# Loading a page table as eight rows and spreading it with a TensorE transpose

## The chip, the cores and the metric

The kernel runs on one core of a Trainium2 chip. The metric is the device time of one execution in microseconds (us). Several executions are timed and their median is given; one more is recorded by the profiler, and that execution has a time and a span of its own. A core has five engines that work side by side, each in the order of its own instruction queue: TensorE (PE in the profile, and PEld for its loads of weights), VectorE (DVE), ScalarE (ACT), GpSimd (POOL) and SyncE (SP, which here only issues transfers). Sixteen DMA engines move the data.

## The reference

One layer of a decoder is computed for a prompt of 1024 tokens and for 8 sequences of 4 new tokens each. Every token goes through a normalisation with a shift and a scale that depend on its sequence, then through two branches: attention with a forget gate (8 heads of 64), and an mLSTM (4 heads of 128). The branches are merged, and an MLP of width 4096 follows. What the change touches is the attention of the 8 short sequences. Their past keys, values and forget gates lie in pages of 128 tokens, and a table says which pages belong to which sequence:

```python
page_table: (8, 4) int32          # 8 sequences, 4 pages each, values 0..39
k_past  = cache_k[layer][page_table].reshape(8, 512, 8, 64)
v_past  = cache_v[layer][page_table].reshape(8, 512, 8, 64)
lf_past = cache_logf[layer][page_table].reshape(8, 512, 8)
fk = cumsum(concatenate([lf_past, a_logf], axis=1), axis=1)   # enters the scores
```

## The kernel before

The kernel keeps the activations as columns (features on the 128 partitions, tokens along the row) and multiplies each weight tile with them in three passes, a high and a low part of each operand (`gemm`, lines 400 to 411). Line 406 multiplies high by high, 407 the high weight by the low activation, 408 the low weight by the high activation. `split_w` (lines 260 to 269) loads a weight tile on SP's queue (L263), makes its high part on ACT (L267) and its low part on DVE or POOL in turn (L268).

**The start.** First the conditioning is multiplied out (`ada_first`, L294, L275). Meanwhile nine tiles of x are loaded on SP's queue (`load_x`, L180) and normalised (`norm_x`: the square on ACT at L310, the rest on DVE and POOL, L312 to L315). `h_part` then transposes x on PE (L336), scales and shifts it out of PSUM on ACT (L341) or DVE (L339), and splits it into a high part on ACT (`Xh`, L348) and a low part on DVE (`Xl`, L349). The h of all tokens is made in three chunks of 352 tokens, each in two halves. The gate products and the first projections run on PE between these parts.

**The order.** The program is written as a sequence of stages: gates, `qkv(0)`, `dprep()`, and then for each of four pairs of heads the attention and the next `qkv`, with further products (`fill`) placed between. A planner lays out each engine's queue when the kernel is built: it goes by priorities that follow the order of the program, with offsets by name, and by a simulated timeline (`TCARGS`). Buffers of a tag go round in the order in which the program asks for them. Two tags matter here. `PT` has two buffers of SBUF; `h_part` uses them for its unsplit half, `dprep` for its two work tiles A and B, and attention for its transposed probabilities. `ps_t`, asked for with `bank("t")`, has two banks of PSUM; the transposes to tokens in `qkv` (L628, read by ACT at L629, and L632), the one in `dprep` (L577) and those of attention (L707, read at L709 and L710) use them in turn.

**`dprep`** turns the table into row numbers. The caches are seen as rows of which 32 (forget gates) or 64 (keys, values) make up a page, so that partition p, with j = p // 32 and r = p % 32, wants row 32 * table[b, j] + r for sequence b. In the kernel before, four loads on SP (L553) bring the table to all partitions, one for each page j: each writes column j of the table, 8 words, to 32 partitions. DVE casts them to float (L556), multiplies and adds the row number (L559), and writes three sets of indices (L560, L562). Eight lookups on POOL (`gather`, L440) then fetch the forget gates into A. A copy (L574), four transposes (L577), a running sum (L579) and some scaling (L578 to L583) end in `nF2`, which the decoding stage needs much later; its lookups of keys and values use the same indices.

Of the kernel before, what the change touches and what calls it, by code (L numbers as in the profile page):

```python
# [11 lines left out]
I32 = mybir.dt.int32  # L12
U32 = mybir.dt.uint32
AF = mybir.ActivationFunctionType
ALU = mybir.AluOpType
# [3 lines left out]
P = 128  # L19
D = 1024  # L20
NP = 1024
NB = 8
TD = 4
ND = NB * TD
T = NP + ND
# [20 lines left out]
PAGES = 4  # L46
# [16 lines left out]
def _mark(nc, label):  # L63
    pass
# [3 lines left out]
def hybrid_kernel(ctx: ExitStack, tc: tile.TileContext, ins, outs):  # L68
    nc = tc.nc
    pe, act, dve, pool, sp = nc.tensor, nc.scalar, nc.vector, nc.gpsimd, nc.sync  # L70
    uid = [0]

    def tl(pl, shape, dt=F32, tag=None, bufs=None):
        uid[0] += 1
        tag = tag or f"u{uid[0]}"
        kw = {} if bufs is None else {"bufs": bufs}
        return pl.tile(list(shape), dt, name=f"{tag}_{uid[0]}", tag=tag, **kw)
# [13 lines left out]
    def f(ap):  # L91
        return ap.bitcast(F32)

    def bc(ap, n):

        return ap.broadcast_to(list(ap.shape[:-1]) + [n])
# [43 lines left out]
    cst = ctx.enter_context(tc.tile_pool(name="cst", bufs=1))  # L140
# [9 lines left out]
    def slot(role, shape, dt=F32):  # L150

        uid[0] += 1
        n, w = {"Pt": (3, KEYS * 2), "PT": (2, T)}.get(role, (1, T))
        t = big.tile([P, w], dt, name=f"{role}_{uid[0]}", tag=role, bufs=n)
        m = 1
        for x in shape[1:]:
            m *= x
        t = t[:shape[0], 0:m]
        if len(shape) == 3:
            t = t.rearrange("p (a b) -> p a b", b=shape[2])  # L160
        elif len(shape) == 4:
            t = t.rearrange("p (a b c) -> p a b c", b=shape[2], c=shape[3])
        return t
# [3 lines left out]
    def bank(tag):  # L167
        return tl(ps, [P, 512], F32, "ps_" + tag, PSB[tag])
# [35 lines left out]
    ident = tl(cst, [P, P])  # L204
# [47 lines left out]
    pt = bank("t")  # L252
# [69 lines left out]
    def h_part(ci, q):  # L322
# [7 lines left out]
        for k in range(4 * q, 4 * q + 4):  # L330
# [15 lines left out]
            if k % 2:  # L346
                k2 = slice(k - 1, k + 1)
                act.copy(hh[:, k2], hf)  # L348
                dve.tensor_sub(hl[:, k2], hf, f(hh[:, k2]))  # L349

    def load_params():
        prow = slot("stg", [120, P])
        act.dma_start(prow[0:48], ins["b_ada"].rearrange("l (r p) -> (l r) p", p=P))
        for i, nm in enumerate(("g_pre_mix", "g_post_mix", "g_pre_mlp", "g_post_mlp")):
            act.dma_start(prow[48 + 8 * i:56 + 8 * i], ins[nm].rearrange("l (r p) -> (l r) p", p=P))
        act.dma_start(prow[80:112], ins["conv_w"].rearrange("l j (r p) -> (l j r) p", p=P))
        act.dma_start(prow[112:120], ins["conv_b"].rearrange("l (r p) -> (l r) p", p=P))
        pt = bank("t")
        pe.transpose(pt[:, :120], prow, ident[:120, :120])
        dve.tensor_copy(prm, pt[:, :120])  # L360
# [17 lines left out]
    for i in range(8):  # L378
        if i == 0:
            load_params()  # L380
        if i >= AW:
            ada_w.append(load_ada(i))
        ada_first(i)
        for _ in range(X_AT[i]):
            x_l.append(load_x(len(x_l)))
            if len(x_l) <= 3:
                norm_x(len(xts))
        for ci in HAT.get(i, ()):
            P_(f"h{ci}0", h_part, ci, 0)
            h_done.append((ci, 0))  # L390
        if i == GW:
            gate_w = P_("gw", load_gate_w)
# [46 lines left out]
    def gather(dst, src, i, b):  # L439
        pool.indirect_dma_start(dst, None, src, bass.IndirectOffsetOnAxis(idx[:, i, b:b + 1], 0))  # L440
# [51 lines left out]
    if True:  # L492
# [39 lines left out]
        for q in range(2):  # L532
            pt = bank("t")
# [6 lines left out]
        pt = bank("t")  # L540
# [5 lines left out]
    def dprep():  # L546

        _mark(nc, "dprep")
        pti = tl(cst, [P, NB], I32)
        rowi = tl(cst, [P, 1], I32)  # L550
        for j in range(PAGES):
            r_ = slice(32 * j, 32 * j + 32)
            sp.dma_start(pti[r_], ins["page_table"][:, j:j + 1].rearrange("b o -> o b").broadcast_to([32, NB]))  # L553
            pool.iota(rowi[r_], [[0, 1]], 0, 1)
        ptf = tl(cst, [P, NB])
        dve.tensor_copy(ptf, pti)  # L556
        rowf = tl(cst, [P, 1])
        dve.tensor_copy(rowf, rowi)
        dve.tensor_scalar(ptf, ptf, 32.0, rowf, ALU.mult, ALU.add)  # L559
        dve.tensor_copy(idx[:, 0], ptf)  # L560
        for i in range(2):
            dve.tensor_scalar(idx[:, 1 + i], ptf, 2.0, float(i), ALU.mult, ALU.add)  # L562

        A = slot("PT", [P, T])
        lfg = A[:, 0:256].rearrange("p (b c) -> p b c", b=NB)
        for b in range(NB):
            gather(lfg[:, b], clf, 0, b)
        lfh = A[:, 256:512].rearrange("p (i h b) -> p i h b", i=4, h=AH)
        nFd = A[:64, 512:512 + KEYS]
        B = slot("PT", [P, T])  # L570
        LR = B[:64, 0:PAST + TD]
        Fd = B[:64, PAST + TD:2 * (PAST + TD)]
        sp.dma_start(LR[:, PAST:], d_lfd.rearrange("h (b t) -> (h b) t", t=TD))
        dve.tensor_copy(lfh, lfg.rearrange("p b (i h) -> p i h b", i=4))  # L574
        pt = bank("t")
        for i in range(4):
            pe.transpose(pt[:64, i * P:(i + 1) * P], lfh[:, i].rearrange("p h b -> p (h b)"), ident)  # L577
        act.copy(LR[:, 0:PAST].rearrange("p (x i) -> p i x", i=4), pt[:64].rearrange("p (i x) -> p i x", i=4))  # L578
        dve.tensor_tensor_scan(Fd, bc(one[:64, 0:1], PAST + TD), LR, 0.0, ALU.mult, ALU.add)  # L579
        act.mul(nFd[:, 0:PAST].rearrange("p (i x) -> p i x", i=4), Fd[:, 0:PAST].rearrange("p (x i) -> p i x", i=4), -1.0)  # L580
        dve.tensor_scalar(nFd[:, PAST:].rearrange("p (b t) -> p b t", t=TD), Fd[:, PAST:].unsqueeze(1).broadcast_to([64, NB, TD]), -1.0, None, ALU.mult)
        act.copy(nF2[0:64], nFd)
        dve.tensor_sub(nF2[64:P], nFd, f(nF2[0:64]))  # L583
# [68 lines left out]

    nxt = qkv(0)
    dprep()
    for fp in range(4):
        heads = nxt
        KL = heads[2]
        _mark(nc, f"attn{fp}")
        if True:
            for hd in range(2):  # L660
# [7 lines left out]
                for j in range(4):  # L668
# [28 lines left out]
                    for m in range(j + 1):  # L697
                        pt = bank("t")
# [175 lines left out]
    if True:  # L874
# [298 lines left out]
        pt = bank("t")  # L1173
# [37 lines left out]
    for q in range(2):  # L1211
        pt = bank("t")
# [267 lines left out]
    for n_, (c, ts) in enumerate(((0, (0, 8, 1, 2, 3)), (1, (0, 8, 1, 2, 3)), (1, (4, 5, 6, 7)), (0, (4, 5, 6, 7)))):  # L1480
        if c not in W:
            W = {c: w_half(c)}
        for i, t in enumerate(ts):
# [4 lines left out]
            with after(last) if t == 8 else nullcontext():  # L1488
                o, last = R.gemm(W[c])
# [38 lines left out]
    def u_out(c, ft, h, eng):  # L1528
        if eng == "A":
            act.activation(c, c, AF.Relu)  # L1530
            act.activation(c, c, AF.Square)
        else:
            dve.scalar_tensor_tensor(c, c, 0.0, c, ALU.max, ALU.mult)
        sp.dma_start(d_u[ft, :, HB[h][0]:HB[h][1]], c)

    def pair(i, hs):
# [54 lines left out]
        for h in hs:  # L1591
            u_out(c1[h], 2 * i, h, "A")

# [155 lines left out]
```

## Time and profile before

| What | Value |
|---|---|
| Median of three runs | 1887.87 us (1885.29 to 1894.61) |
| The profiled execution's own time | 1890.58 us |
| Its span, from the first to the last instruction | 1888.6 us |
| PE busy | 1813.9 us (96% of the span) |
| DVE busy | 996.0 us (53%) |
| ACT busy | 819.6 us (43%) |
| POOL busy | 423.6 us (22%) |
| Mean granted clock of TensorE | 0.981 |
| Moved by DMA | 211.80 MB, mean 112 GB/s |

In the profile a line such as `DVE u L556 <- DMA u<-in_page_table: 10.9, 1, 10.9` says who waited (DVE, at line 556, writing a tile named u), for whom (a transfer from the page table), for how many microseconds in total, how often, and how long at the longest. Small constants have names of the form u and a number, and the profile shows them all as u. A row of a table by stretches has the busy time of PE, PEld, DVE, ACT and POOL in that stretch, each with its number of instructions, and then the clock that TensorE was granted (1.00 is full speed), the mean busy share of the sixteen DMA engines, and GB/s.

### The profile page before, as it was taken

To read this page: it belongs to the slowest core of one execution; us is meant where nothing else is said; L and a number is where in the kernel's file an instruction comes from. 1 tells how busy PE (TensorE), PEld (TensorE's weight loads), DVE (VectorE), ACT (ScalarE), POOL (GpSimd) and SP (SyncE) were. 2 spreads that over 40 slices of the span, in tenths; PEclk is the share of its full clock that TensorE was granted. 3 is DMA by queue.
4 is the path that set the end of the run, shared out by engine and by line. 5 is a ranking of instruction groups with operands and counts; after the bars stand their busy time and mean duration, and the time that the engine had idled before them with its cause. 6 is when DMAs were issued, how large, how long until landed. Compare 5 with 4: busy or idle time off the path is not lost. (4 is left out here: it accounts for less than half of the span.)

```text
span 1888.6 us, 29922 instructions
## 1 busy us (share of the span) xinstructions
PE 1813.9 (96%) x11871; PEld 1683.3 (89%) x11871; DVE 996.0 (53%) x1927; ACT 819.6 (43%) x1424; POOL 423.6 (22%) x337
## 2 busy tenths in 40 slices
PE   6899999999999999999999978999998999999997
PEld 3799789998888999979898767899998899999997
DVE  3554555554446555554454487756457424444436
ACT  4556546556556434443132666444445431111201
POOL 3200010000233111111143243444443211111113
PEclk9999999999999999989899988999999999999998
DMA  8321432122556312164234343433344522222223
GB/s 276 79 70 61 143 90 79 51 78 93 170 190 214 93 52 69 32 209 153 68 102 131 127 135 95 121 104 109 103 152 145 157 94 92 91 91 91 91 62 123
DMA packets 203381, 211.80 MB, mean 112 GB/s; under 512 B 14589, under 2 KB 170809, under 8 KB 203242
## 3 DMA queue, kind: packets, MB, share of 16 engines
q1 hardware_dynamic: 198154, 192.92, 32.3%
q0 software_dynamic: 4864, 16.91, 2.7%
q8 instruction: 93, 1.52, 0.3%
q14 instruction: 46, 0.38, 0.1%
q10 hardware_dynamic: 224, 0.06, 0.0%
HBM read 166.16 MB, written 43.70 MB: 111 GB/s over the span
## 5 line engine op out<-in xcount | busy, mean ns | idle before, releaser
L406 PE MATMUL ps_g<-Xh,wh 128*128 128x352 f32 (+1 forms) x1176 | 392.3, 334 | 0.2 <-ACT Xh L348 0.2
L408 PE MATMUL ps_g<-Xh,wl 128*128 128x352 f32 (+1 forms) x1176 | 389.4, 332 | 0.2 <-DVE wl L268 0.2
L407 PE MATMUL ps_g<-Xl,wh 128*128 128x352 f32 (+1 forms) x1080 | 355.0, 329 | 1.2 <-DVE Xl L349 1.1
L406 PEld LDWEIGHTS ps_g<-Xh,wh 128*128 128x128 f32 (+1 forms) x1176 | 221.8, 189 | 6.0 <-issue 3.0
L408 PEld LDWEIGHTS ps_g<-Xh,wl 128*128 128x128 f32 (+1 forms) x1176 | 220.9, 188 | 6.3 <-issue 4.5
L406 PE MATMUL ps_g<-R,wh 128*128 128x352 f32 x672 | 217.7, 324 | 1.8 <-ACT wh L1255 1.7
L408 PE MATMUL ps_g<-R,wl 128*128 128x352 f32 x672 | 218.5, 325 | 0.0
L407 PE MATMUL ps_g<-R,wh 128*128 128x352 f32 x672 | 217.6, 324 | 0.0
L407 PEld LDWEIGHTS ps_g<-Xl,wh 128*128 128x128 f32 (+1 forms) x1080 | 202.5, 188 | 7.3 <-issue 4.0
L268 POOL TENSOR_TENSOR wl<-wr,wh 128x1024 fp32r<-128x1024 f32 x26 | 62.7, 2410 | 433.1 <-ACT wh L267 371.9
L1647 DVE TENSOR_TENSOR acc<-acc,ps_g 128x352 f32<-128x352 f32 x144 | 74.6, 519 | 151.0 <-PE ps_g L408 151.0
L1256 POOL TENSOR_TENSOR wl<-wr,wh 128x1024 fp32r<-128x1024 f32 (+1 forms) x43 | 101.0, 2352 | 229.9 <-ACT wh L1255 223.6
L1255 ACT CAST wh<-wr 128x1024 fp32r<-128x1024 f32 (+1 forms) x63 | 61.2, 975 | 194.8 <-PE ps_g L407 148.0
L406 PEld LDWEIGHTS ps_g<-R,wh 128*128 128x128 f32 x672 | 126.2, 188 | 2.4 <-ACT wh L1255 1.9
L408 PEld LDWEIGHTS ps_g<-R,wl 128*128 128x128 f32 x672 | 126.5, 188 | 0.0
L407 PEld LDWEIGHTS ps_g<-R,wh 128*128 128x128 f32 x672 | 126.1, 188 | 0.0
L683 DVE CUSTOM_DVE_ANT_0 Pt<-ps_s,nF 128x384 f32<-128x384 f32 (+4 forms) x96 | 51.7, 554 | 65.2 <-PE ps_t L707 39.6
L267 ACT CAST wh<-wr 128x1024 fp32r<-128x1024 f32 x52 | 54.5, 1048 | 72.0 <-PE ps_g L407 54.1
L1256 POOL TENSOR_TENSOR wl<-wx,wh 128x512 fp32r<-128x512 f32 (+1 forms) x18 | 35.5, 1975 | 186.2 <-ACT wh L1255 184.5
L1255 ACT CAST wh<-S 128x1024 fp32r<-128x1024 f32 x44 | 46.3, 1052 | 40.3 <-PE ps_g L1519 17.9
L709 ACT CAST PT<-ps_t 128x512 fp32r<-128x512 f32 (+1 forms) x80 | 40.5, 545 | 53.1 <-PE ps_t L707 52.6
L690 ACT ACTIVATE Pt<-Pt,nm 128x128 f32<-128x128 f32 (+3 forms) x64 | 49.7, 777 | 31.8 <-DVE nm L688 20.8
(714 smaller groups left out, 4560.7 us busy)
## 6 DMA issues: line engine op xcount, KB each, us to landing
wr<-in_w_in SPq DMA_DIRECT2D x44, 512.0 KB
wr<-in_w_up SPq DMA_DIRECT2D x33, 512.0 KB
R<-d_u SPq DMA_DIRECT2D x32, 528.0 KB
wr<-in_w_ada SPq DMA_DIRECT2D x32, 512.0 KB
wr<-in_w_down SPq DMA_DIRECT2D x24, 512.0 KB
d_sg<-sgo SPq DMA_DIRECT2D x60, 176.0 KB
d_u<-n SPq DMA_DIRECT2D x32, 272.0 KB
d_u<-n SPq DMA_DIRECT2D x32, 256.0 KB
```

The lines of the kernel that those rows point to most:

```text
L267: act.copy(wh, wr)
L268: (dve if lo_turn[0] % 2 else pool).tensor_sub(wl, wr, f(wh))
L406: pe.matmul(o, wh[:, k], rh(k, a, b), start=(k == 0), stop=False)
L407: pe.matmul(o, wh[:, k], rl(k, a, b), start=False, stop=False)
L408: last = pe.matmul(o, wl[:, k], rh(k, a, b), start=False, stop=(k == nk - 1))
L683: dve.tensor_tensor_reduce(Pt[:, k0:k1], s_, nF[:, k0:k1], 1.0, -3.0e38, ALU.add, ALU.max, mx[:, pi:pi + 1])
L690: act.activation(Pt[:, :nk], Pt[:, :nk], AF.Exp, bias=nm, accum_out=sm)
L709: act.copy(PTh[:, :w_], pt[:, :w_])
L1255: act.copy(h_, src)
L1256: (pool if on_pool else dve).tensor_sub(l_, src, f(h_))
L1647: dve.tensor_tensor(accs[a // 352](ft), accs[a // 352](ft), o, ALU.add)
```

## The change

The table is loaded as it lies in memory, eight rows of four words, in one transfer on ACT's queue at the head of `load_params`. In `dprep` DVE casts it to float and repeats each of the four entries 32 times along the row, which gives 8 rows of 128 in the upper part of work tile A. A transpose on PE makes of this 128 partitions of 8, in a bank of the tag "t". The multiplication and addition reads that bank; the index operations behind it are as they were. The four loads and the cast behind them are gone. Work tile A is asked for earlier in the program, and one more "t" bank is asked for.

```diff
+    pg = tl(cst, [NB, PAGES], I32)
+
     def load_params():
+        act.dma_start(pg, ins["page_table"])
         prow = slot("stg", [120, P])
...
     def dprep():
-        pti = tl(cst, [P, NB], I32)
         rowi = tl(cst, [P, 1], I32)
         for j in range(PAGES):
             r_ = slice(32 * j, 32 * j + 32)
-            sp.dma_start(pti[r_], ins["page_table"][:, j:j + 1].rearrange("b o -> o b").broadcast_to([32, NB]))
             pool.iota(rowi[r_], [[0, 1]], 0, 1)
         ptf = tl(cst, [P, NB])
-        dve.tensor_copy(ptf, pti)
         rowf = tl(cst, [P, 1])
         dve.tensor_copy(rowf, rowi)
-        dve.tensor_scalar(ptf, ptf, 32.0, rowf, ALU.mult, ALU.add)
+        A = slot("PT", [P, T])
+        pgx = A[:NB, 900:900 + P]
+        dve.tensor_copy(pgx.rearrange("b (j r) -> b j r", r=32), bc(pg.unsqueeze(2), 32))
+        pt = bank("t")
+        pe.transpose(pt[:, 0:NB], pgx, ident[:NB, :NB])
+        dve.tensor_scalar(ptf, pt[:, 0:NB], 32.0, rowf, ALU.mult, ALU.add)
         dve.tensor_copy(idx[:, 0], ptf)
...
-        A = slot("PT", [P, T])
         lfg = A[:, 0:256].rearrange("p (b c) -> p b c", b=NB)
```

## The prediction

> **What bounds the kernel now.** I read the page first, for the shares of the engines.
>
> ```profile
> span 1888.6 us, 29922 instructions
> PE 1813.9 (96%) x11871; PEld 1683.3 (89%) x11871; DVE 996.0 (53%) x1927; ACT 819.6 (43%) x1424; POOL 423.6 (22%) x337
> ```
>
> PE is the bound: 1888.6 - 1813.9 = 74.7 us of the span are PE idle, and only what shortens these, or PE's work at a low clock, shortens the kernel. Then I cut the span into stretches of 60 us, to see where the idle time lies.
>
> ```profile
> 0.00:60.00 60.00, 37.09 (x184) 20.73 (x184) 22.66 (x61) 25.45 (x41) 16.65 (x39) 0.89 0.80 252
> 60.00:120.00 60.00, 58.69 (x365) 55.28 (x366) 37.85 (x79) 37.27 (x57) 14.37 (x12) 1.00 0.24 64
> 120.00:180.00 60.00, 60.00 (x373) 54.89 (x371) 29.54 (x83) 37.17 (x63) 2.39 (x1) 1.00 0.19 64
> ```
>
> The first column after the stretch is its length, the next PE's busy time; the last three are the granted clock, the DMA share and GB/s. The first 60 us hold 60 - 37.09 = 22.9 us of PE idle, more than any other stretch, and the page table is read there. From 60 us on PE is nearly never short of work. So I asked for the waits of the first 130 us, engine by engine (DVE's, PE's and ACT's own lists; total, times, longest).
>
> ```profile
> DVE u L556 <- DMA u<-in_page_table: 10.9, 1, 10.9
> PE ps_t L336 <- DVE PT L339: 7.6, 1, 7.6
> ACT stg L310 <- DMA Pt<-in_x_prompt: 9.5, 1, 9.5
> ```
>
> The three longest waits of the three engines are one event. The timeline of SP, DVE, PE and ACT (start, length, instruction, idle before it and its releaser) puts it in order:
>
> ```profile
> 37.97 1.26 SPq L263 DMA_DIRECT2D wr<-in_w_in  x2
> 39.28 2.88 SPq L553 DMA_DIRECT2D u<-in_page_table  x4
> 42.27 1.14 SPq L180 DMA_DIRECT2D Pt<-in_x_prompt  x2
> 43.46 5.12 SPq L180 DMA_DIRECT2D Pt<-in_x_sample  x1
> ...
> 54.01 0.17 DVE L556 CAST u<-u 128x8 f32<-128x8 int32 x1 [10.87 <-DMA u<-in_page_table]
> 54.12 0.64 DVE L339 TENSOR_SCALAR PT<-ps_t,mod,mod 128x352 f32<-128x352 f32 x1
> ...
> 46.88 0.33 PE L406 MATMUL ps_g<-Xh,wh 128*72 128x352 f32 x1
> 54.82 0.48 PE L336 MATMUL ps_t<-u,KB 128*128 128x128 f32 x1 [7.62 <-DVE PT L339]
> ...
> 44.95 1.17 ACT L341 ACTIVATE PT<-ps_s,mod,mod 128x352 f32<-128x352 f32 x2
> 55.67 1.06 ACT L310 ACTIVATE stg<-Pt 128x1024 f32<-128x1024 f32 x1 [9.54 <-DMA Pt<-in_x_prompt]
> ```
>
> DVE works in order. The cast of the page table (L556) stands in its queue at 43.1 us and waits 10.87 us. Behind it stand the two evacuations L339 of the transposed x; PE runs out at 47.2 and waits 7.62 us for them. ACT waits 9.54 us for a tile of x that SP issued just behind the page table. What the DMA did meanwhile:
>
> ```profile
> 39.00:43.00 4.00, 2.29 (x10) 1.69 (x10) 3.12 (x6) 3.18 (x7) 1.64 (x2) 0.50 1.05 254
> 43.00:50.00 7.00, 4.20 (x23) 3.34 (x21) 0.15 (x2) 2.54 (x4) 2.94 (x2) 0.89 0.08 7
> 50.00:54.00 4.00, 0.00 (x0) 0.00 (x0) 0.00 (x0) 0.00 (x0) 0.00 (x0) 0.67 0.76 233
> 54.00:58.00 4.00, 3.18 (x15) 2.80 (x15) 3.99 (x11) 2.33 (x4) 0.33 (x1) 0.50 0.64 139
> ```
>
> For 7 us, from 43 to 50, it moved 7 GB/s at a share of 0.08, which is about one of the sixteen engines, while the last piece of x stood in SP's queue with an issue of 5.12 us. That is the page table going over in single words, four loads of 256 words of 4 bytes, and x does not pass it. The clock then falls to 0.50 and PE restarts slowly.
>
> **The change, step by step.** *The four loads go.* They free 2.88 us of SP and the 7 us of nearly empty DMA. In their place one load of eight rows of 16 bytes goes out first on ACT's queue, at the start of the kernel; it is needed only after the h stage, so it is hidden. It delays ACT's queue by about one small issue of ACT's:
>
> ```profile
> 8.44 0.28 ACTq L364 DMA_DIRECT2D u<-in_b_fox_f  x1
> ```
>
> I take 0, with 0.3 us as the upper end, if a parameter load behind it should be on the path.
>
> The Trainium skill (DMA: Bandwidth & Descriptors, Rules for kernel authors) says that a last dimension which isn't contiguous is sent as one descriptor per element; the 7 us stretch agrees. The same page (Anatomy of one DMA) fits a DMA that GpSimd issues by 2.0 us plus bytes over 436 GB/s, and by that the four loads would have landed near 44 us, my estimate, and their removal would be worth about 1 us, a time near 1887. The 10.87 us of the row decide against it.
>
> *DVE's wait goes.* DVE runs L339 at 43.2 and PE finds its bank at 47.2: 7.62 us. What is late next is ACT, whose L348 cast stands behind L310, the square of the late tile of x. That tile is now issued at about 39.4 and follows the two weight tiles of 512 KB that SP issued at 37.97. How those landed:
>
> ```profile
> 42.36 1.05 ACT L267 CAST wh<-wr 128x1024 fp32r<-128x1024 f32 x1 [0.77 <-DMA wr<-in_w_in]
> 44.00 1.05 ACT L267 CAST wh<-wr 128x1024 fp32r<-128x1024 f32 x1 [0.59 <-DMA wr<-in_w_in]
> ```
>
> They came 44.00 - 42.36 = 1.64 us apart, so a third of this size lands at 45.6, before ACT is free (44.95 + 1.17 = 46.1), and ACT moves by its whole 9.54 us. The other end: in the profile the tile released ACT 5.7 us after the transfers had picked up again at 50; counted from 43.5 that gives 49.2, and a shift of 55.67 - 49.2 = 6.5 us. From 47 to 60 PE, ACT and DVE hand each other tiles of h, so the stage moves by ACT's shift, between 6.5 and 9.5; the words still draining explain part of the 5.7, so I stand nearer the weights' rows: 8.5 us. A PE that stays at full clock is counted in it, as its work there is not the last to end.
>
> *The index work moves.* New on DVE is one cast of 8 x 128, new on PE one transpose with 8 columns out; the two index operations behind them stay. Nearest rows:
>
> ```profile
> 112.41 0.23 PE L541 MATMUL ps_t<-u,stg 72*32 72x72 f32 x1
> 54.68 0.22 DVE L559 TENSOR_SCALAR u<-u,u 128x8 f32<-128x8 f32 x1
> ```
>
> The cast replaces a cast. PE pays 0.1 to 0.3, I take 0.2. POOL's four index rows stay.
>
> *The lookups start later.* This is the price that the profile doesn't show. The transpose takes a bank of the two "t" banks, which go round in program order: its turn comes after the token transposes of the first qkv, and its bank is the one that ACT's L629 gives back. So idx is ready only after that, and the eight lookups with it:
>
> ```profile
> 72.17 1.62 POOL L440 DMA_INDIRECT PT<-in_cache_logf,u  x1 [10.44 <-DVE Xl L349]
> 81.87 0.94 POOL L440 DMA_INDIRECT PT<-in_cache_logf,u  x1 [0.30 <-issue]
> 85.31 0.86 DVE L574 COPY PT<-PT 128x256 f32<-128x256 f32 x1 [1.97 <-DMA PT<-in_cache_logf,u]
> ...
> 121.71 1.08 ACT L629 COPY stg<-ps_t 128x512 f32<-128x512 f32 x2 [1.65 <-PE ps_t L628]
> 125.74 0.60 PE L577 MATMUL ps_t<-u,PT 128*64 128x128 f32 x4
> 130.81 0.47 ACT L709 CAST PT<-ps_t 128x384 fp32r<-128x384 f32 x1
> ```
>
> The first and the last of the eight are shown. On the clock of before: bank free at 121.71 + 1.08 = 122.8, transpose and three index operations to about 124, lookups and landing as now 85.31 - 72.17 = 13.1 us, copy 0.9: L577 at 138.0 in place of 125.74, 12.3 us late. Attention's first L709 writes the same PT buffer, and moves from 130.81 to about 139. Queued behind it on PE, ACT and DVE is the rest of the first head. The cover is the second qkv and the gate products: PE is busy for all 60 us of 120 to 180, POOL for 2.39 of them, so the eight lookups (about 10.6 us of POOL) find it free. With cover the delay costs PE nothing; without it, up to 12.3 us. Nothing excludes a small gain, as the lookups leave 72 to 83, but PE was full there: lower end 0. I take 1.3, for one wait in order on L574 and L577 of the size of the 1.97 us that L574 shows now: the fill is nearest, since the rows show full cover.
>
> *Sum.* The profiled execution took 1890.58 us, span 1888.6 and 2.0 around it. 1890.58 - 8.5 + 0.2 + 1.3 = 1883.6. It stands 2.7 above the median of the runs, 1887.87, so for a median I say 1881. The instruction order is laid out anew at build time, over the whole kernel, by a planner that works with a simulated timeline; I add +-4 us for that, an estimate from the 10.6 us that PE idles between 60 and 1080 and that a new order can make or lose in part:
>
> ```profile
> 60.00:1080.00 1020.00, 1009.37 (x6423) 911.53 (x6424) 539.11 (x1291) 502.69 (x917) 182.72 (x182) 0.99 0.34 106
> ```
>
> **Rivals.** *The lookups cost more than the stall (slower).* At 12.3 us with no cover: 1887.87 - 8.5 + 0.2 + 12.3 = 1892. It decides from the point where over 8.3 us of the delay arrive at the end of the kernel. For it: the fills are a fixed stock, and those run early are missing later. Against it: PE is full from 120 to 180, and the 1080 us stretch above has only 1% idle. Of a slowing of the lookups themselves, beside a busy DVE, the value lookups are the row:
>
> ```profile
> L440 POOL DMA_INDIRECT VB<-in_cache_v,u x5: 933/954/1469, 510.8 to 606.3; - x5
> ```
>
> min, median and max are 933, 954 and 1469 ns, against 0.95 us for most of the eight now: at the worst 8 x 0.5 = 4 us more, which makes 1896. The Trainium skill (SBUF — State Buffer, SBUF: two separate sides) tells of a transfer issued by GpSimd that grew from about 620 to 3100 ns beside a DVE copy; by five times, my estimate, the chain would be 30 us later still and the time over 1910. The medians do not bear that out, and I give it 1 in 100. All together 13 in 100.
>
> *More comes off.* All of DVE's 10.87 us, with a PE that never cools: 1887.87 - 10.87 - 1 = 1876. For it: PE runs at 0.50 from 54 to 58, 3.18 us of work that would take half. Against it: ACT's 9.54 is less. 17 in 100.
>
> *x is late anyway.* If ACT's tile comes no earlier, PE gets its bank at 47.2 but stands again until the L348 behind L310: 1887. For it: 5.7 us from pick-up to release. Against it: the transfer was not moving from 43 to 50 at all. 10 in 100.
>
> **How the numbers follow.** The forecast, 1881 with its own range 1877 to 1886, has 60 in 100. The range of all, 1871 to 1893, takes in the larger gain less the planner's 4 us, x late, and the delay without cover. Half a per cent, about what a measurement of this kernel can tell from no change, is 9.4 us: faster begins below 1878.4. The larger gain is faster (0.17), and a quarter of the forecast (0.15): 0.32. Slower begins above 1897.3: only the upper part of the slower rival, with the planner's 4 us on top, gets there: 0.08. Rest: 0.60.
>
> **What would show it.** After the change no wait of DVE for the page table; SP goes from the weights straight to x; no stretch of 7 us under 10 GB/s; PE resumes at 47 to 48 and the clock stays at 1.00 from 45 on; the end of the h stage some 8 us earlier. The transpose of the table behind the second L629 on vT, the lookups near 115 to 126, L577 near 130, and PE still full there. Wrong would make it: a PE wait of several us on L577 or L709, PE idle added late in the mLSTM stage, or the same 55.67 for ACT's L310.

## The result and the profile after

| | before | after |
|---|---|---|
| Median of the runs | 1886.58 us (1881.49 to 1894.61) | 1919.65 us (1908.1 to 1921.1) |
| The profiled execution | 1890.58 us, span 1888.6 us | 1921.1 us, span 1919.4 us |
| Mean granted clock | 0.981 | 0.964 |

The ratio after to before is 1.0155 (95% interval 1.0119 to 1.019). In a later round with more runs it was 1.0085 (1.0048 to 1.0122). The forecast was 1881 us, in a range of 1871 to 1893: the change makes the kernel slower, by 0.85% to 1.55%, and the range missed it. Lines from 351 on stand three or four higher in the changed kernel, so L577 is now L581 and L683 is L687; in the experiments they move by a few more.

The page's head, for the span and PE's busy time:

```profile
span 1919.4 us, 29941 instructions
PE 1839.5 (96%) x11872; PEld 1702.3 (89%) x11872; DVE 995.8 (52%) x1927; ACT 829.7 (43%) x1432; POOL 424.0 (22%) x337
```

PE is busy for the same 96%, but for 25.6 us more at a lower clock. Now the waits of the first 130 us by engine (total, times, longest):

```profile
DVE u L363 <- PE ps_t L362: 12.2, 1, 12.2
DVE PT L578 <- DMA PT<-in_cache_logf,u: 11.6, 1, 11.6
...
PE ps_t L336 <- DVE PT L339: 1.3, 1, 1.3
...
ACT stg L310 <- PE ps_t L362: 7.3, 1, 7.3
```

DVE's 10.87 us for the page table are gone. One row further down stands a new wait of the same size, 11.6 us, now for the lookups. The first part went as forecast, as the timeline of SP, DVE, ACT and PE shows (start, length, instruction, idle before it):

```profile
36.74 1.30 SPq L263 DMA_DIRECT2D wr<-in_w_in  x2
38.15 1.71 SPq L180 DMA_DIRECT2D Pt<-in_x_prompt  x2
39.90 0.56 SPq L180 DMA_DIRECT2D Pt<-in_x_sample  x1
...
43.41 0.64 DVE L339 TENSOR_SCALAR PT<-ps_t,mod,mod 128x352 f32<-128x352 f32 x1
44.55 1.06 ACT L310 ACTIVATE stg<-Pt 128x1024 f32<-128x1024 f32 x1 [0.59 <-DMA Pt<-in_x_prompt]
...
45.91 0.27 PE L336 MATMUL ps_t<-u,KB 128*128 128x128 f32 x1
...
61.56 1.70 DVE L349 TENSOR_TENSOR Xl<-PT,Xh 128x704 fp32r<-128x704 f32 x2 [0.70 <-ACT Xh L348]
```

x goes out directly behind the weights, ACT has its tile at 44.55 in place of 55.67, the transposes L336 for which PE had waited run at 45.91 in place of 54.82, and the last split of h starts 9.4 us earlier than before. This is the kernel before, with three rows more that are used further down:

```profile
70.97 1.70 DVE L349 TENSOR_TENSOR Xl<-PT,Xh 128x704 fp32r<-128x704 f32 x2 [0.70 <-ACT Xh L348]
...
122.81 0.43 DVE L647 CAST VA<-stg 128x512 fp32r<-128x512 f32 x1 [5.74 <-ACT stg L629]
...
137.31 0.41 DVE L720 TENSOR_TENSOR oT<-ps_o,oT 64x256 f32<-64x256 f32 x1
...
511.44 0.43 DVE L720 TENSOR_TENSOR oT<-ps_o,oT 64x256 f32<-64x256 f32 x1
```

Each L720 row is the end of one step of attention: four pairs of heads, two heads in a pair and four steps in a head make 32. The first of the two ends the first step, the second the last one. After the change (POOL, DVE and PE in one list):

```profile
116.36 0.22 DVE L564 TENSOR_SCALAR u<-ps_t,u 128x8 f32<-128x8 f32 x1
...
116.87 0.23 DVE L567 TENSOR_SCALAR u<-u 128x8 uint32<-128x8 f32 x2
117.25 1.24 POOL L443 DMA_INDIRECT PT<-in_cache_logf,u  x1 [17.45 <-DVE u L567]
...
126.29 0.94 POOL L443 DMA_INDIRECT PT<-in_cache_logf,u  x1 [0.30 <-issue]
128.70 0.40 DVE L578 COPY PT<-PT 128x256 f32<-128x256 f32 x1 [11.61 <-DMA PT<-in_cache_logf,u]
130.88 0.60 PE L581 MATMUL ps_t<-u,PT 128*64 128x128 f32 x4
131.63 0.69 DVE L687 CUSTOM_DVE_ANT_0 Pt<-ps_s,nF 128x512 f32<-128x512 f32 x1 [2.53 <-PE ps_t L711]
...
145.28 0.41 DVE L724 TENSOR_TENSOR oT<-ps_o,oT 64x256 f32<-64x256 f32 x1
...
536.03 0.43 DVE L724 TENSOR_TENSOR oT<-ps_o,oT 64x256 f32<-64x256 f32 x1
```

The index is ready at 117.1, the lookups run from 117.25 to 127, and DVE stands from 117.1 to 128.7 at the copy L578. Behind it in DVE's queue are the row maxima L687 of attention, and behind L581 in PE's queue the transposes L711 that those wait for. The first step of attention ends at 145.28, 8.0 us later than before although h was 9.4 us earlier. I call the sum of the two, 17.4 us, the hold. It is not yet the loss: at the end of the first pair of heads the lag behind the kernel before is 5.4 us (223.97 against 218.52), and only over the other three pairs does it grow to 24.6 us.

Where it was paid shows in the windows (PE's busy time is the second number, the granted clock the third from the end). Before:

```profile
180.00:250.00 70.00, 68.72 (x479) 55.78 (x479) 42.23 (x118) 39.37 (x78) 4.79 (x2) 1.00 0.47 141
420.00:540.00 120.00, 117.04 (x761) 103.50 (x761) 52.61 (x144) 68.51 (x118) 23.00 (x32) 0.99 0.45 143
900.00:960.00 60.00, 60.00 (x338) 53.67 (x338) 28.60 (x87) 11.07 (x22) 10.44 (x9) 0.89 0.24 71
```

The same stretches after the change, and the one of the hold ahead of them:

```profile
120.00:180.00 60.00, 60.00 (x371) 55.22 (x370) 24.12 (x70) 39.19 (x60) 8.04 (x7) 1.00 0.16 53
180.00:250.00 70.00, 64.77 (x390) 50.00 (x389) 39.02 (x105) 32.10 (x66) 5.41 (x2) 0.83 0.47 139
420.00:540.00 120.00, 111.03 (x689) 96.62 (x689) 53.86 (x146) 73.04 (x123) 18.62 (x20) 0.93 0.39 123
900.00:960.00 60.00, 60.00 (x294) 54.24 (x292) 21.72 (x62) 9.69 (x24) 8.54 (x6) 0.72 0.28 87
```

And PE's longest wait from 180 to 250 us after the change (total, times, longest):

```profile
PE ps_g L470 <- DMA wr<-in_w_ada: 3.3, 3, 2.0
```

During the hold itself PE was full: 60.00 of 60 us from 120 to 180, at clock 1.00. It ran other products, which stand there in its queue since the kernel was built. The bill came at the turn from the first pair of heads to the second and at the end of attention. Busy time times clock is an estimate of the work done: at 180 to 250 us 68.7 before and 53.8 after (14.9 lost), at 420 to 540 us 115.9 and 103.3 (12.6 lost), at 900 to 960 us 53.4 and 43.2 (10.2 lost). Less the 9.4 gained in the h stage that is 28.3 us; the spans differ by 30.8.

The planner laid out another order with it. I compared PE's matmuls in order of start, line by line, with those of the kernel before (times here are on its clock). From 57 to 121 us the order is the same, through all of attention it is another, and from 539 us to the end it is again the same, matmul for matmul.

### The profile page after: what moved, and what is told of

The parts are those of the page before. It is cut to its first block, busy times and chain, and to the rows that moved or that the text cites. A ratio compares the mean times of both kernels' runs of the same rounds, so it can differ in the third digit from the quotient of the medians.

```text
span 1919.4 us, 29941 instructions
## 1 busy us (share of the span) xinstructions
PE 1839.5 (96%) x11872; PEld 1702.3 (89%) x11872; DVE 995.8 (52%) x1927; ACT 829.7 (43%) x1432; POOL 424.0 (22%) x337
## 5 line engine op out<-in xcount | busy, mean ns | idle before, releaser
L409 PE MATMUL ps_g<-Xh,wh 128*128 128x352 f32 (+1 forms) x1176 | 396.4, 338 | 1.4 <-ACT wh L267 1.1
L410 PEld LDWEIGHTS ps_g<-R,wh 128*128 128x128 f32 x672 | 126.3, 188 | 0.0
L687 DVE CUSTOM_DVE_ANT_0 Pt<-ps_s,nF 128x384 f32<-128x384 f32 (+4 forms) x96 | 51.4, 554 | 69.0 <-PE ps_t L711 47.3
L1522 PE MATMUL ps_g<-R,wh 128*128 128x256 f32 (+1 forms) x176 | 51.6, 296 | 12.9 <-ACT v L1565 5.9
L1259 ACT CAST wh<-S 128x1024 fp32r<-128x1024 f32 x44 | 46.3, 1052 | 40.5 <-PE ps_g L1523 17.9
L1260 POOL TENSOR_TENSOR wl<-S,wh 128x1024 fp32r<-128x1024 f32 x20 | 52.5, 2637 | 46.7 <-ACT wh L1259 46.6
```

The source lines that it names most:

```text
L409: pe.matmul(o, wh[:, k], rh(k, a, b), start=(k == 0), stop=False)
L410: pe.matmul(o, wh[:, k], rl(k, a, b), start=False, stop=False)
L687: dve.tensor_tensor_reduce(Pt[:, k0:k1], s_, nF[:, k0:k1], 1.0, -3.0e38, ALU.add, ALU.max, mx[:, pi:pi + 1])
L1259: act.copy(h_, src)
L1260: (pool if on_pool else dve).tensor_sub(l_, src, f(h_))
L1522: pe.matmul(o, wh[:, k], xh[:, k], start=first and k == 0, stop=False, skip_group_check=True)
```

## The experiments

**The theories.** L: the turn of the bank "t" makes the lookups late, and whatever waits for them holds attention; without the lateness the gain of the h stage remains. P: the planner's new order, or the clock, loses the time somewhere, whatever the lookups do. Inside L stand two ways: through the two PT buffers, or through the order of the queues. There is a third reading between L and P, which no experiment was made for: the late lookups make the planner lay out another order for attention, and that order loses the time. The two columns on the right bear on it.

| kernel | eight lookups, us | hold, us | ratio to before (95% interval) | PE's order as before from, us | last step of attention, us later |
|---|---|---|---|---|---|
| changed | 117.2 to 126.3 | 17.4 | 1.0155 (1.0119 to 1.019) | 539 | 24.6 |
| after_again | 123.5 to 132.6 | 17.9 | 1.0085 (1.0048 to 1.0122) | 539 | 28.0 |
| e1_bank_o | 103.2 to 112.3 | -0.4 | 0.9953 (0.9926 to 0.998) | 120 | -2.4 |
| e2_late_only | 125.8 to 134.8 | 17.7 | 1.0113 (1.0077 to 1.0149) | 539 | 32.2 |
| e3_loads_early | 75.2 to 84.9 | 0.3 | 1.0003 (0.9973 to 1.0034) | 57 | 3.5 |
| e4_split | 119.4 to 128.5 | -2.4 | 1.0077 (1.0042 to 1.0112) | 539 | 23.0 |
| e5_load_behind | 97.7 to 106.8 | 0.2 | 0.9942 (0.9917 to 0.9967) | 120 | -9.6 |
| e6_index_first | 107.4 to 116.4 | 3.9 | 0.9934 (0.9908 to 0.996) | 236 | -7.4 |
| e7_no_lookups | none | 3.9 | 0.9968 (0.9943 to 0.9994) | 251 | -1.2 |
| e8_stock | 117.6 to 126.6 | 18.0 | 1.0078 (1.0048 to 1.0109) | 945 | 19.0 |
| e9_first_stock | 106.5 to 115.5 | 3.6 | 1.0038 (1.0013 to 1.0062) | 945 | 12.3 |
| e10_first_twice | 106.1 to 127.0 (sixteen) | 17.3 | 1.0089 (1.0058 to 1.0119) | 539 | 22.4 |
| e11_free_buffers | 117.6 to 126.6 | 15.6 | 1.0073 (1.0044 to 1.0102) | 539 | 20.9 |
| e12_first_free | 105.5 to 114.6 | 1.9 | 0.9939 (0.9907 to 0.9971) | 159 | -1.7 |
| e13_behind_two | 119.8 to 128.8 | -2.3 | 0.9954 (0.9927 to 0.9982) | 236 | -6.9 |

The times of the lookups are the starts of the first and the last. The hold is worked out as above, from the L349 and the L720 of each trace. Each ratio is against runs of the kernel before on the same chip. The fifth column is the point, on the clock of the kernel before, from which at least 2300 matmuls of PE come line for line in its order; in e8 and e9 the unit that was added to the fills also shifts the order up to 945 us, and behind 900 us some of the others have short stretches in another order. The last column compares the last L720 with the 511.44 of before. Both are from one profile of each kernel.

**e1_bank_o.**

```diff
-        pt = bank("t")
+        pt = bank("o")
         pe.transpose(pt[:, 0:NB], pgx, ident[:NB, :NB])
```

> The changed kernel, but the transpose of the table goes to a PSUM bank of the tag o in place of t. Theory L (late lookups: the bank t puts the eight lookups behind the token transposes of the first qkv, attention's first head is then held, and the products that fill it are missing later): the lookups go back to 62 to 75 us, L581 (the four transposes behind them) to about 116, and the gain of the h stage, 9.4 us, stays to the end: 1878 us, 1872 to 1884, against 1887 for the kernel before. Theory P (the loss lies in a new instruction order or in dips of the clock anywhere in the span, whatever the lookups do): 1900 or more, or a value between with no relation to the time of the lookups.

The ratio is that of L's 1878 over 1887. The lookups did not go back to 62 to 75 us, as the bank "o" also has a queue of users; 103 us was early enough for no hold at all. One word of the code takes the loss away, with the transpose still in place, and PE's order is that of before from 120 us on.

**e2_late_only.** The loads of the kernel before, and beside them:

```diff
+        zz = A[:NB, 900:900 + P]
+        dve.memset(zz, 0.0)
+        pt = bank("t")
+        pe.transpose(pt[:, 0:NB], zz, ident[:NB, :NB])
...
+        dve.tensor_tensor(ptf, ptf, pt[:, 0:NB], ALU.add)
```

> The kernel before with its four loads of columns, and only the lateness added: a tile of zeros is transposed into a t bank and added to the index, so that the lookups wait for that bank as in the changed kernel. Theory L: the stall of the h stage stays (VectorE's wait of about 10.9 us for the table), the lookups come at 115 us or later, and the time is the 1920 of the changed kernel plus what the h stage gained there, up to 9 us: 1925, range 1912 to 1935. Theory P: the lookups are late too, but the time is 1880 to 1900, as nothing holds the end.

1916.96 us: the lateness alone, without the new load, costs 1.1% and makes the same hold. P's 1880 to 1900 is out, and with it that the lookups don't matter; PE's order through attention is another here too, so that an order that comes from the lateness is not out. L's size was a little high.

**e3_loads_early.** The four loads at the head of `load_params`, no transpose:

```diff
     def load_params():
+        for j in range(PAGES):
+            act.dma_start(pti[32 * j:32 * j + 32], ins["page_table"][:, j:j + 1].rearrange("b o -> o b").broadcast_to([32, NB]))
```

> The kernel before with its four loads of columns unchanged in form, but issued at the head of load_params on ScalarE's queue, with no transpose. PE's order is that of the kernel before. Theory L: the stall of the h stage goes, the lookups stay at 62 to 75 us, and the time is 1878 us, 1872 to 1886; up to 5 us more if the single words hold up the loads of the parameters behind them at the start. Theory P: no fixed expectation, 1872 to 1920, with the clock windows telling.

No gain (1.0003), where L had said 1878 us. The stall moved to the start: ACT's queue issues the last of its four gain vectors at 16.54 us, where before it was at 3.5. From ACT's timeline:

```profile
4.36 0.32 ACTq L355 DMA_DIRECT2D u<-in_page_table  x1
4.71 1.53 ACTq L357 DMA_DIRECT2D stg<-in_b_ada  x1
...
16.54 0.28 ACTq L359 DMA_DIRECT2D stg<-in_g_post_mlp  x1
```

And DVE still waits for the table, as its list of waits over the first 110 us says:

```profile
DVE u L558 <- DMA u<-in_page_table: 8.3, 1, 8.3
```

The last split of h then starts 3.0 us later than before. So the words were slow at both places, and the single load of eight rows is worth having.

**e4_split.** The lookups write into a free part of the tile oT, and

```diff
+            if fp == 0:
+                dprep2(lfg_)
             if fp < 3:
                 nxt = P_("q", qkv, fp + 1)
```

where `dprep2` holds what follows the lookups, in PT buffers as before.

> The changed kernel with its t bank, so the lookups stay late at about 117 us, but they write to a free part of another tile (oT), and what follows them (the copy into the PT buffers, the four transposes, the running sum) is called after the attention of the first two heads. So attention does not queue behind the lookups. Theory L with blocked buffers as the cause: 1878 to 1886. If the late lookups themselves cost the time (their place beside other work on GpSimd and DMA): 1905 or more. Theory P: anywhere from 1880 to 1920.

Both expectations missed in part. The first pair of heads ran 8 to 10 us earlier than before, with lookups at 119 us: late lookups by themselves hold nothing. But 1.0077 remains. The next step of attention, behind `dprep2`, is 3.1 us later than before and the last one 23.0 us. At the new place of `dprep2` PE waits 2.7 us for weights and the clock falls, and the end of attention loses as in the changed kernel, in its windows:

```profile
220.00:230.00 10.00, 7.19 (x38) 4.26 (x36) 4.62 (x16) 3.34 (x8) 0.00 (x0) 0.61 0.95 291
230.00:240.00 10.00, 10.00 (x42) 6.27 (x42) 5.50 (x16) 6.34 (x12) 3.46 (x2) 0.50 0.66 179
420.00:540.00 120.00, 108.86 (x682) 94.30 (x681) 54.74 (x142) 73.37 (x120) 19.56 (x21) 0.93 0.40 127
```

So there is a kernel with no hold that has another order through attention, and its loss of 0.77% is near the 0.85% of the changed one in the later round.

**after_again and after_third.** The changed kernel, unaltered.

> The changed kernel once more, unaltered, beside the others of this round, so that its loss is known on the same chip and with more runs: 1.5% over the kernel before by the first comparison, and a like dip of the clock at 205 to 245 us if that belongs to the order of the work. If the dip at 930 to 955 us belongs to chance, it is elsewhere or shorter in this profile.

> One more look at the changed kernel, unaltered, for its clock. Two profiles of it have 0.83 and 0.85 at 180 to 250 us and 0.72 and 0.74 at 900 to 960 us. If both dips belong to the order of the work they are here again; one that is chance is not.

after_again has a median of 1908.43 us (1904.02 to 1927.43) and after_third took 1907.92 us. The third profile has these windows:

```profile
180.00:250.00 70.00, 63.88 (x396) 48.81 (x396) 38.76 (x103) 32.24 (x67) 5.46 (x2) 0.85 0.46 139
420.00:540.00 120.00, 109.61 (x690) 94.96 (x689) 54.59 (x149) 74.13 (x124) 17.69 (x19) 0.93 0.38 121
900.00:960.00 60.00, 60.00 (x348) 54.45 (x347) 28.07 (x80) 12.23 (x27) 10.68 (x8) 0.89 0.33 102
```

PE's order is the same in all three profiles. The first two losses are there in each of them; the clock at 180 to 250 us was 0.83, 0.85 and 0.85. The third is 0.72, 0.74 and 0.89, the 0.89 being that of the kernel before: about 10 us that come in some executions and not in others, and most of the way from 1908 to 1921. The gain of the h stage varies too. In after_again it is 3.6 us, and in after_third 7.8:

```profile
67.37 1.69 DVE L349 TENSOR_TENSOR Xl<-PT,Xh 128x704 fp32r<-128x704 f32 x2 [0.70 <-ACT Xh L348]
```

What differs ahead of it is PE's pace: from 20 to 40 us it ran 81 matmuls in after_again, 96 in after_third and 105 in the first profile.

**e5_load_behind.** The bank "o", and the load goes behind the loads of the gate bias:

```diff
         act.dma_start(bias[64:68], ins["b_ml_i"].rearrange("l h -> h l"))
+        act.dma_start(pg, ins["page_table"])
```

> The bank o as in the first experiment, and the load of the eight rows is moved from the head of load_params to behind the loads of parameters and of the gate bias on ScalarE's queue. In the changed kernel and in the first experiment TensorE's transpose of the parameters (L362) came at 19.66 us in place of 15.75, and the first experiment kept only 3.9 us of the gain at 100 us. If the load at the head of the queue did that, the transpose goes back to about 15.8 us and the gain at 100 us grows to 8 us or more: 0.5% below the first experiment's ratio of 0.995, so 0.990 (0.987 to 0.994). If the start varies by itself from execution to execution, 0.995 as before.

The transpose of the parameters came at 15.52 us and the gain at the last split of h is 9.1 us, as said, but the ratio of 0.9942 is not below that of the first experiment by anything that can be told. So the expectation's other branch is the nearer one: the 3.6 us of e1 belong to its one profiled execution, as the 3.6 of after_again do, and e7, e8 and e11, with the load at the head of the queue like e1, gain 8.6 to 9.7 us. The gain does arrive at the end: 0.58% of 1893 us is 11 us.

**e6_index_first.** Bank "t" again, the load as in e5, and

```diff
-    nxt = qkv(0)
-    dprep()
+    ag = dprep()
+    nxt = qkv(0)
+    dprep2(*ag)
```

> The load behind the parameters, as in the experiment beside it, the transpose in a bank of t as in the changed kernel, but the index and the eight lookups are called ahead of qkv(0), so that the turn of the bank comes before the token transposes. Theory L: what cost the time in the changed kernel is the turn of the bank, not the bank: lookups at 60 to 90 us, L581 at about 116, ratio 0.990 (0.987 to 0.996). If a t bank for the table costs by itself, or the planner's order goes wrong for another reason: 1.000 or more.

0.9934, the best ratio of all; 1877.8 us against 1893.05 in its round, faster than both kernels. The lookups came only at 107 us, later than expected, and DVE waits almost as long as in the changed kernel, 10.49 us, in its timeline:

```profile
118.81 0.40 DVE L581 COPY PT<-PT 128x256 f32<-128x256 f32 x1 [10.49 <-DMA PT<-in_cache_logf,u]
...
120.26 0.42 DVE L654 CAST VA<-stg 128x512 fp32r<-128x512 f32 x1
```

The two stretches in its windows:

```profile
180.00:250.00 70.00, 68.34 (x476) 55.51 (x476) 40.50 (x113) 38.73 (x77) 4.79 (x2) 1.00 0.48 149
420.00:540.00 120.00, 115.40 (x759) 100.48 (x758) 54.15 (x141) 70.75 (x122) 27.03 (x37) 1.00 0.45 145
```

The same wait costs almost nothing here, and it ends at 118.8. What stands next in the queue, the cast of V, waited 5.74 us for ACT in the kernel before and started at 122.81. Ten microseconds later the same wait stands in front of attention. With a hold of only 3.9 us, and PE's order as before from 236 us on, the clock stays at 1.00 in both stretches.

**e7_no_lookups.** This kernel leaves out the eight lookups and sets the tile that they fill to zero, so that the decoding is computed with wrong forget gates.

```diff
         for b in range(NB):
-            gather(lfg[:, b], clf, 0, b)
+            pass
+        dve.memset(lfg, 0.0)
```

> The changed kernel without the eight lookups of forget gates (the tile that they fill is set to zero): the turn of the bank and the index stay as late as they are, at about 116 us, only the wait behind them goes. Theory L with the wait for the lookups as the cause: L581 at about 116, attention 0 as in the kernel before or 8 us earlier, ratio 0.990 to 0.998. If the late bank turn itself holds the work (the transposes to tokens, the order of the plan), the ratio stays above 1.008.

0.9968 beside the changed kernel's 1.0085 in the same round: the late bank and the late index cost nothing that shows here without the wait behind them.

**e8_stock and e9_first_stock.** In the changed kernel, and in e6:

```diff
-FILL = {'b1': 'sss', ...
+FILL = {'b1': 'ssss', ...
```

> The changed kernel, with one unit of gate products (a product of about 12 us of TensorE) more among the fills that run beside attention 0 (b1: four in place of three; the list of units is the same, so a late fill is one short). The stock theory: the hold of attention 0 was covered, but by work meant for 200 to 250 us, and the price came there (clock 0.83 and 5 us idle). With one unit more, the clock at 180 to 250 us returns to 0.95 or more, and a good part of the loss comes back: 8 to 15 us less than the changed kernel, ratio about 1.002 (0.998 to 1.005) against 1.0085 and 1.0155. If the loss has another cause (the order, the bank), the ratio stays at 1.008 or above.

> The same unit more in the kernel with the index ahead of qkv(0), which has no hold. The stock theory: nothing to repair, 0.9934 within 0.003. If one unit more helps this kernel by as much as the changed one, the gain is a better fill and says nothing on the late lookups: 0.988 or less.

The window of e8 in the first of the stretches:

```profile
180.00:250.00 70.00, 69.04 (x474) 55.66 (x473) 43.73 (x120) 44.22 (x82) 2.82 (x1) 1.00 0.42 132
```

Two windows of e9:

```profile
180.00:250.00 70.00, 69.05 (x432) 54.70 (x431) 31.64 (x92) 33.59 (x68) 0.92 (x1) 0.88 0.37 119
900.00:960.00 60.00, 60.00 (x279) 53.41 (x279) 24.00 (x74) 8.28 (x23) 8.28 (x7) 0.66 0.24 72
```

One unit more repairs the first stretch of the changed kernel, as the stock theory says: 69.04 us at 1.00 in place of 64.77 at 0.83. But the total (1.0078) is no better than that of the changed kernel, and the same unit makes e6 a whole per cent slower. For the total that is against the stock theory as it was put: its 0.998 to 1.005 didn't come, and 420 to 540 us still has 112.39 us busy at 0.93. It shows that P is right in one thing: a shift of the fills by one unit loses a per cent by itself, as e9 does with a hold of 3.6 us.

**e10_first_twice.** In e6:

```diff
         for b in range(NB):
             gather(lfg[:, b], clf, 0, b)
+        for b in range(NB):
+            gather(lfg[:, b], clf, 0, b)
```

> The kernel with the index ahead of qkv(0), with its eight lookups issued twice over into the same tile. Each set takes 9 to 10 us of GpSimd, so the last lands at about 126 us in place of 117, and attention 0 is held by 9 to 12 us, without any bank asked for late. Theory L: a loss of the size of the hold, 9 to 20 us: ratio 0.9985 to 1.004 against 0.9934. If late lookups as such cost nothing and only the late bank does: 0.9934 within 0.003.

The other side of e7: no bank asked for late, only the last lookup at 127.0 in place of 116.4, and the hold is 17.3 us and the loss against e6 1.55% (1.0089 less 0.9934, about 29 us), more than I expected. PE's order is another through attention, and here PE was not full in the hold (56.61 of 60 us from 120 to 180). DVE's wait, in its list, is hardly longer than in e6; it ends 10.6 us later, at 129.4:

```profile
DVE PT L583 <- DMA PT<-in_cache_logf,u: 11.0, 1, 11.0
```

**e11_free_buffers and e12_first_free.** In the changed kernel, and in e6:

```diff
-        A = slot("PT", [P, T])
+        A = oT[:, 3]
...
-        B = slot("PT", [P, T])
+        B = oT[:, 2]
```

> The changed kernel, with its late bank and its lookups at about 117 us, but dprep's work tiles A and B lie in parts of another tile (oT, rows 2 and 3, not in use before the third pair of heads), so attention's PT buffers don't wait for them. If the hold goes through the PT buffers: attention's first L713 at about 122 to 125 us on the clock of the trace in place of 135, clock above 0.95 at 180 to 250 us, ratio 0.990 to 0.997. If it goes through the order of the queues: L713 near 135 again and a ratio above 1.006.

> The kernel with the index ahead of qkv(0) and the load behind the parameters, with A and B in oT as in the other run. It has no hold, so the buffers should bring nothing: 0.9934 within 0.003. If it gains over 0.4% more, the buffers are worth something by themselves, and a gain of the other run is read less that much.

It isn't the buffers. e11 still loses 0.73% and still holds 15.6 us, with attention's first L713 at 132.8 us and DVE's wait as it was in the list of waits:

```profile
DVE oT L578 <- DMA oT<-in_cache_logf,u: 11.6, 1, 11.6
```

e12 is e6 within the measurement, so free buffers bring nothing by themselves.

**e13_behind_two.** The late bank and the late lookups of the changed kernel, work tiles in oT, and the waiting instructions moved in the order of the program:

```diff
                 for j in range(4):
+                    if fp == 0 and hd == 0 and j == 2:
+                        dprep2(lfg_)
```

> The changed kernel with its late bank and its lookups at about 117 us; the copy of what they bring, the four transposes and the running sum are called behind the first two of the four steps of attention's first head, in buffers of oT. If the order of VectorE's and TensorE's queues is the way in which the late lookups hold attention: no wait of VectorE for the lookups of more than 3 us, attention's first step as early as in the kernel before or some 8 us earlier, ratio 0.991 to 0.998. If the lookups cost by something else (their place beside other transfers, the bank): 1.006 or more.

0.9954. The lookups are the latest but two of the table, and nothing is held. DVE's timeline:

```profile
121.89 0.69 DVE L692 CUSTOM_DVE_ANT_0 Pt<-ps_s,nF 128x512 f32<-128x512 f32 x1 [2.28 <-PE ps_t L716]
...
131.28 0.40 DVE L581 COPY oT<-oT 128x256 f32<-128x256 f32 x1
```

and its windows:

```profile
180.00:250.00 70.00, 68.64 (x478) 55.80 (x477) 40.56 (x115) 40.43 (x79) 4.79 (x2) 1.00 0.48 149
420.00:540.00 120.00, 117.83 (x773) 102.42 (x772) 56.21 (x147) 72.95 (x125) 27.06 (x39) 1.00 0.46 150
```

The row maxima run at 121.89 and the copy comes when its data are there, without a wait. Both stretches are back at full clock. Of the two ways inside L this decides for the order of the queues. Every kernel with a hold over 15 us lost 0.7% to 1.6%; of the nine others six gained, one was level (e3, with its stall at the start), and two lost (e4, e9).

**What the experiments leave open.** That late lookups bring the loss when the instructions that wait for them stand in front of attention is shown both ways: by adding them (e2, e10) and by taking them or their lateness away (e1, e6, e7), or by moving what waits (e13). Whether the wait itself costs the time, or the order that the planner laid around it, is not shown. The table's fifth column is the closer companion of the loss: each kernel that lost has another order all the way to 539 us or more, and no other kernel has. e4 and e9 have another order with a hold of -2.4 and 3.6 us, and lost; no kernel has a hold over 15 us with the order of before.

## Why the prediction was wrong

*The four loads go, DVE's wait goes: right, with a size that varies.* ACT's tile was expected at 45.6 and came at 44.55; the h stage moved by 9.4 us, against 8.5 (6.5 to 9.5). In the two later profiles of the same kernel it moved by 3.6 and 7.8, so that the range holds in two of three. No wait for the table is left, SP goes from the weights to x.

*The load at the head of ACT's queue at 0 to 0.3 us: too low at its place, not at the end.* The transpose of the parameters came 3.9 us later (19.66, before 15.75) in the changed kernel and in e1, since four products L294 that wait 3.18 us for weights now stand ahead of it in PE's order. In the first profile this was made up by 70 us. The kernels with the load at the head gained 3.6 to 9.7 us in the h stage, those with it behind the parameters (e5, e6, e9, e10, e12) 8.9 to 10.1; no difference of it shows in the ratios of e1 and e5.

*The index work at 0.2 us: the size is right.* The new transpose L563 takes 0.22 us of PE, and the two index rows shown above 0.22 and 0.23 us of DVE.

*The lookups start later: the place was right, the price was the step that failed.* The lookups were expected at 115 to 126, L577 near 130 and 12.3 us late; they ran from 117.25 to 127, L581 stood at 130.88, and the delay against the h stage was 5.1 + 9.4 = 14.5 us. The term of the sum for it was 1.3 us, from "with cover the delay costs PE nothing" and a wait on L574 "of the size of the 1.97 us". e6 and e13, which keep the load and the transpose without the hold, put it at 0.9934 and 0.9954 against 1.0085 to 1.0155: at least 1.0085 - 0.9954 = 1.3%, 25 us.

Two things were wrong in that step. The wait of 1.97 us was measured in a queue in which the lookups had long been under way; with the lookups last, the copy waits for all eight and their landing, 11.61 us. The prediction names what stands behind it ("the rest of the first head") and then prices only the waiting instruction. And the cover was taken from PE's busy share during the delay, 60.00 of 60. That was true after the change too, and so were the lookups at 117 us and L581 at 130.88, as forecast; a full PE at that place couldn't show the loss. The products that covered the delay are missing later, where PE then waits for weights (3.3 us at 180 to 250) and is given less clock. For the first stretch e8 supports this, where one unit of products more brought back the clock and the busy time, though not the total.

A second term failed beside it: the +-4 us for the planner, taken from the 10.6 us that PE idled between 60 and 1080 us. No kernel with the order of before lost; in the changed kernel, with the other order, PE idles 1020 - 1000.06 = 19.9 us over the same stretch, and the granted clock there is 0.96 in place of 0.99. How much of the 25 us belongs to this term and how much to the wait stays open.

*The slower rival* named this mechanism ("the fills are a fixed stock, and those run early are missing later"), with a price of at most 12.3 us and 13 in 100. The price was no upper bound: the last step of attention is 24.6 us late, and the granted clock fell in the stretches that lost. What "lookups slowed by a busy DVE" would have made, up to 4 us, wasn't there: in the changed kernel each takes about 0.94 us but the first, beside a DVE that stands still, and in e13, where DVE is busy for 4.2 of the 10 us from 119.8 on, they take 0.94 to 0.95 us as well.

*Of the Trainium skill's estimates* the prediction set aside the one from DMA: Bandwidth & Descriptors (Anatomy of one DMA), by which the removal would be worth about 1 us; the 3.6 to 9.4 us of the h stage are for setting it aside. The 1 in 100 for the factor of five from SBUF — State Buffer (SBUF: two separate sides) was right to be small, by the durations of e13.

What stays open: how the loss at 420 to 540 us follows from late lookups 300 us earlier. All the kernels with a hold have it, e6 and e13 don't. But e4 has it too, without a hold and with another order of PE's queue, so the order is the nearer suspect. No run holds attention with the order of before, and none has the other order with everything else as it was.

## What to carry to other kernels

When a step makes data late, look up the instruction that waits for them in its engine's queue, and price what stands behind it; if it can't be made early, move the waiting instruction behind work that is ready, which here turned a loss of 0.85% to 1.55% into a gain of 0.46% (e13; e4, which moved it further back, lost). Where a planner lays out the queues, compare the order of the instructions of the two kernels before anything else is blamed: here every kernel that lost had another order through attention. A PE that is full during a delay doesn't prove that the delay is free; look at the next stretch that is short of work. A long wait that was free in one place (10.49 us in e6) went with a loss of over 20 us some ten microseconds later.

## What the runs showed of the hardware

The granted clock carried more of the loss than idle time did: PE's idle time grew by 4.0 and 6.0 us in the two stretches, the lost clock was worth about 11 and 7 more. A dip came without a long wait too: in e12, with a hold of 1.9 us, PE waited 0.6 us for weights at 180 to 250 us, and it has these two windows there:

```profile
220.00:230.00 10.00, 9.43 (x40) 5.22 (x41) 5.27 (x20) 4.05 (x10) 0.00 (x0) 0.56 0.75 242
230.00:240.00 10.00, 10.00 (x44) 6.62 (x45) 3.18 (x10) 4.51 (x8) 2.36 (x1) 0.50 0.44 116
```

PE reads as busy in the second, 10.00 of 10, with 44 matmuls, and 81 in the ten microseconds ahead of the two. The Trainium skill (TensorE: Matmul & The Clock Gate, HAM oscillation — how this bites in real kernels) says that waits for DMA make the clock fall back to half rate, and its next section (A second HAM failure mode: psum-queue depth-cycling) that frequent short idle gaps between groups of matmuls do so too. The windows at 0.50 agree with half rate, and the waits for weights in the changed kernel and in e4 with the first; which gaps did it in e12 no run shows. The same stretch of the same kernel can have such a dip in one execution and not in the next (0.72, 0.74, 0.89 at 900 to 960 us in the changed kernel), so a busy share says nothing without the clock beside it, and a difference between two single profiles of 10 us can be one dip. Nor does the clock column always show it: in after_again it reads 1.00 from 20 to 30 us, while the twenty products L294 that begin there with the tile Xl take 1.06 us each, against 0.59 us for the shortest of them in the first profile.
